# One power for four tiles in the band's query and key norm, and two gate products issued beside the last heads

## The chip, the cores and the metric

The kernel runs on one core of a Trainium2 chip. The metric is the device time of one execution in microseconds (us), the median of three runs. The engines are named as in the profile: PE is TensorE (its matmuls; PEld its weight loads), DVE is VectorE, ACT is ScalarE, POOL is GpSimd, SP is SyncE, which issues most DMAs.

## What is computed

Two transformer layers act on one sequence of 512 tokens with width 1024. The change lies in the second layer, whose mixer has two halves of width 512:

```python
qa, ka, va, qkv_b, z_b, b_raw, a_raw = jnp.split(proj, cuts, axis=-1)
o_a = chunked_band_attention(qa, ka, va, q_gain, k_gain, rel_bias)   # 8 heads of 64, rms norm of q and k per head
o_a = rms_norm_2(o_a, attn_out_gain)
o_b = gated_delta_rule(q_b, k_b, v_b, g, beta)                       # 4 heads of 128
o_b = rms_norm_2(o_b, dn_out_gain) * jax.nn.silu(z_b)                # z_b: the gate
mix = jnp.concatenate([o_a, o_b], axis=-1) @ w_out
x = x + gate1 * mix
```

The norm of q and k is x times (mean(x*x) + eps) to the power -0.5, for each token and head. After this a mixture of 16384 single-neuron experts follows, which takes the second half of the kernel's time.

## The kernel before

Activations lie as 512 tokens in four tiles of 128 (`NT = 4`). Large products run in three passes of a rounded format: each weight block of 128x1024 numbers is loaded (SP queue, four buffers `wr`), rounded to a high part `wh` on ACT (L51) and its remainder `wl` computed on DVE, or on POOL where the caller passes `eng` (L52; three buffers each). `gemm_t` (L76) then issues 24 matmuls of 512 columns (L72 to L74) into one of four PSUM buffers named `g`. `gemm_n` (L87) gives the four tiles side by side, with a callback `mid` every second tile (L98 to L100).

Every engine executes its instructions in a fixed order. That order isn't the order of the text: a planner reorders at build time. It takes, on each engine, the instruction that stands earliest in the text among those that its own estimate of times shows ready and for which a buffer is free. On the chip the engine then waits wherever an instruction isn't ready, with all that is queued behind it.

The stages around the change, in the order of the text:

- `band_pre` (L1176) makes the band's q (j=0) and k (j=1). For each, a `gemm_n` of 512 columns, then per tile: copy to SBUF on ACT (L1201), square (L1203) and sum (L1205) on DVE, scale and eps (L147, in `rstd_small`), power on POOL (L151; tiles `bn_v`, `bn_r`, one buffer each), and the product on DVE (L1207). After j=1 a `gemm_n` of 256 columns for the values (`w_va1`). The transposes of the normed tiles are L1188.
- `dn_tile` (L997), two of them at once (tiles 2 and 3), are steps that `mid` releases between the products of `band_pre`: each call of `mid(n)` adds n to a debt and issues one step for each whole unit of it. There are 19 steps; twelve of them alternate L1064 (a product with `Ub`, which POOL makes, L1060), copies and transposes (L1066, L1053, L1054), and L1073 with a subtraction on DVE into `X` (L1074), on which the next L1064 waits. The last one is L1078 to L1086. The debts sum to 18 by the end of `band_pre`; what is left follows in a loop (L916).
- `dn_scan` (L1100), twelve steps, and `band` (L1215), 32 steps, are issued in turn, two of the band for one of the scan. A step of the band is one tile of one head: scores into a buffer `g` (L1230), `soft` (L543): maximum on DVE (L548), exponential on ACT (L552), reciprocal and product on DVE (L554, L555), transposes on PE (L559), copy on ACT (L561), product with the values on PE (L563). Every second head ends with a copy (L1235), a square on ACT (L204) and a sum on POOL (L206). After the scan eight steps are left, the last two heads. The band's end is a sum over channels (L114), a power (L151), a broadcast (L136, L138) and four products (L1241).
- `zb` (L1088) makes the four gate products, `gemm_t` of `w_zb`, with a tanh on ACT (L1094) and a product on DVE (L1096) each. The text issues the first after the band's end; `pair` (L243) then splits the band's four results, `dn_out` (L1162) transposes and gates the scan's (L1170, L1172), between the other three; then `out2` (L1249) multiplies with `w_o2`.

Of the kernel before, what the change touches and what calls it, by code (L numbers as in the profile page):

```python
# [8 lines left out]
F32 = mybir.dt.float32  # L9
# [6 lines left out]
OP = mybir.AluOpType  # L16
AX = mybir.AxisListType
# [3 lines left out]
P = 128  # L21
T = 512
NT = 4
# [3 lines left out]
class Kernel:  # L27
# [860 lines left out]
    def layer2(self, st0):  # L888
        tc, nc, I = self.tc, self.nc, self.i
        cp, mod2 = self.cp, self.mod2  # L890
        with ExitStack() as st:
            lp = self.lp = st.enter_context(tc.tile_pool(name="lp", bufs=1, reuse_waits="tile"))
            G = self.gains[0]
            nc.vector.scalar_tensor_tensor(G, mod2[:, 8:16], 1.0, G, op0=OP.add, op1=OP.mult)
            with tc.tile_pool(name="hp2", bufs=1, side="right", reuse_waits="tile") as hp:
                hs = [(self.t(hp, [P, T], F32R, f"hh{k}"), self.t(hp, [P, T], F32R, f"hl{k}")) for k in range(8)]
                with tc.tile_pool(name="np2", bufs=1, reuse_waits="tile") as np2:
                    self.norm_mod(np2, self.x1, hs, G, mod2[:, 0:8], self.ss)
                sd = ExitStack()
                self.dk = sd.enter_context(tc.tile_pool(name="dk", bufs=1, reuse_waits="tile"))  # L900
                with tc.tile_pool(name="dp", bufs=1, reuse_waits="tile") as self.dp:
                    self.dn_pre(hs)
                    for _ in self.dn_tiles([0, 1]):
                        pass
                    tiles = self.dn_tiles([2, 3])
                    self.owed = 0.0

                    def mid(n):

                        self.owed += n  # L910
                        while self.owed >= 1.0:
                            self.owed -= 1.0
                            next(tiles, None)

                    self.band_pre(hs, mid)
                    for _ in tiles:  # L916
                        pass
                with tc.tile_pool(name="bp", bufs=1, side="right", reuse_waits="tile") as bp:
                    self.bp = self.ap = bp
                    scan, band = self.dn_scan(), self.band()  # L920
                    zb = self.zb(hs)
                    for _ in scan:
                        next(band)
                        next(band)
                    for _ in band:
                        pass
                    next(zb)
                    parts = [self.pair(bp, x, "pr", "pts", 4) for x in self.oa]
                    out = self.dn_out()
                    for _ in zb:  # L930
                        next(out)
                    for _ in out:
                        pass
                    sd.close()
                    self.out2(parts)
# [152 lines left out]
    def zb(self, hs):  # L1088
        nc = self.nc
        self.zzb = []  # L1090
        for h in range(4):
            z = self.gemm_t(self.i["w_zb"][h], 8, hs)
            tz = self.t(self.bp, [P, T], F32, "tz", 2)
            nc.scalar.activation(tz, z, AF.Tanh, scale=0.5)  # L1094
            zz = self.t(self.lp, [P, T], F32, f"zzb{h}")
            nc.vector.scalar_tensor_tensor(zz, tz, 1.0, z, op0=OP.add, op1=OP.mult)  # L1096
            self.zzb.append(zz)
            yield
# [77 lines left out]
    def band_pre(self, hs, mid):  # L1176
        nc, I, lp, dp = self.nc, self.i, self.lp, self.dp
        G = nc.gpsimd
        gq = self.load(dp, "attn_qk_g", [P, 2])
        nc.vector.tensor_scalar(gq[:, 0:1], gq[:, 0:1], 0.125, None, op0=OP.mult)  # L1180
        sh = [P, 8, 64]
        self.aT = [self.t(self.ep, [P, 4, T], F32, f"e{j}") for j in range(2)]

        def trans(j, xs):
            for t in range(NT):
                p = self.t(self.pa, [P, T], F32, "a")
                for b in range(4):
                    nc.tensor.transpose(p[:, b * P:b * P + P],  # L1188
                                        xs[t][:, 2 * b:2 * b + 2].rearrange("p h d -> p (h d)"), self.ident)
                nc.scalar.activation(self.aT[j][:, :, t * P:t * P + P], p.rearrange("p (b x) -> p b x", b=4), AF.Copy,  # L1190
                                     scale=gq[:, j:j + 1])

        xs = None
        for j, w in enumerate(("w_qa", "w_ka")):
            ps = self.gemm_n(I[w], 512, hs, mid=lambda: mid(0.8))
            if j:
                trans(0, xs)
            xs = []
            for t in range(NT):
                x = self.t(dp, sh, F32, "cv_u" if t % 2 else "cv_t", 2)  # L1200
                nc.scalar.activation(x, ps[t].rearrange("p (h d) -> p h d", h=8), AF.Copy)  # L1201
                sq = self.t(dp, sh, F32, "qn_d", 1)
                nc.vector.tensor_mul(sq, x, x)  # L1203
                s = self.t(dp, [P, 8], F32, "bn_s", 2)
                nc.vector.tensor_reduce(s, sq, axis=AX.X, op=OP.add)  # L1205
                r = self.rstd_small(dp, s, 1.0 / 64, "bn")
                nc.vector.tensor_mul(x, x, r.unsqueeze(2).to_broadcast(sh))  # L1207
                xs.append(x)
        ps = self.gemm_n(I["w_va1"], 256, hs, mid=lambda: mid(0.65))
        for t in range(NT):  # L1210
            nc.scalar.activation(self.va[:, t, 256:], ps[t], AF.Copy)
        with self.tc.issue_after(self.mm.ins):
            trans(1, xs)
# [514 lines left out]
def host_layout(inp):  # L1728
# [47 lines left out]
    w2 = a["w_in_2"][0]  # L1776
    o = np.cumsum([0, 512, 512, 512, 1536, 512, 4, 4])
    qa, ka, va, qkv, zb, b_, a_ = [w2[:, o[j]:o[j + 1]] for j in range(7)]
    r["w_va0"] = wn(np.concatenate([va[:, :256], b_, a_], 1))
    r["w_va1"] = wn(va[:, 256:])  # L1780
    r["w_qa"], r["w_ka"] = wn(qa), wn(ka)
    r["w_qkv"], r["w_zb"] = wt(qkv), wt(zb)
    r["dn_conv"] = np.ascontiguousarray(a["dn_conv_w_2"][0].reshape(4, 12, P).transpose(2, 1, 0))
    r["dn_dt_bias"], r["dn_a_log"] = row(a["dn_dt_bias_2"][0]), row(a["dn_a_log_2"][0])
# [34 lines left out]
```

## Time and profile before

| | before |
|---|---|
| median of three runs | 2485.56 us (2482.98 to 2485.98) |
| profiled execution, its time | 2485.87 us |
| profiled execution, its span | 2483.2 us |
| PE busy | 2391.6 us, 96% of the span |
| DVE, ACT, POOL busy | 75%, 42%, 28% |
| granted TensorE clock, mean | 0.989 |
| `band_pre` | about 960 to 1076 us |
| scan and band | about 1076 to 1159 us |
| gate products and `out2` begin | 1140 us and 1177 us |

The span is what lies between the first and the last instruction; 2.7 us of the execution lie around it. A busy PE isn't a PE at its peak: a matmul counts as busy for as long as it lasts, also at half clock. The granted clock of a stretch is the mean of its two levels, 1.0 for 2.4 GHz and 0.5 for 1.2 GHz.

### The profile page before, as it was taken

The page shows a single profiled execution, that of the slowest core. Times are in us where ns is not written, and L with a number is a line of the kernel's source. Part 1 is how long each engine was busy: PE and PEld are TensorE (multiplying, and loading weights), DVE is VectorE, ACT ScalarE, POOL GpSimd, SP SyncE. Part 2 cuts the span into 40 slices and gives each one's busy share as a digit, 9 for nine tenths or more (in the row PEclk, how much of TensorE's full clock was granted, in tenths as well). Part 3 has the DMA queues.
Part 4 walks back from the last instruction along what each step waited for, and adds up shares of the span by engine and source line. Part 5 has one row for each costly group of instructions (what it writes and reads, how often), then busy time and mean ns, then how long its engine had stood idle before and what let it go on. Part 6 is the DMA issues. An engine that isn't in the chain of part 4 may idle for free.

```text
span 2483.2 us, 34683 instructions
## 1 busy us (share of the span) xinstructions
PE 2391.6 (96%) x12573; PEld 2021.0 (81%) x12573; DVE 1867.6 (75%) x3610; ACT 1046.0 (42%) x1871; POOL 704.4 (28%) x526
## 2 busy tenths in 40 slices
PE   5998999999999999999999999999999999999999
PEld 4786777778788778876788999999978888888887
DVE  7895677777765575565458889989668888888887
ACT  3444466653322434354444344454433333333332
POOL 0250111120000112421344665211224344444431
PEclk9999999999999999999999999999999999999999
DMA  7222212228865310111422565889989999999996
GB/s 258 77 85 77 77 55 82 81 73 292 291 224 192 122 68 31 39 60 47 134 77 85 191 198 184 299 310 340 324 278 345 342 348 347 350 348 335 354 353 245
DMA packets 197579, 497.66 MB, mean 200 GB/s; under 512 B 19872, under 2 KB 83872, under 8 KB 194336
## 3 DMA queue, kind: packets, MB, share of 16 engines
q1 hardware_dynamic: 157088, 336.06, 39.9%
q0 software_dynamic: 36864, 134.23, 14.9%
q10 hardware_dynamic: 3456, 25.17, 2.6%
q8 instruction: 98, 1.61, 0.3%
q14 instruction: 73, 0.60, 0.1%
HBM read 446.63 MB, written 48.76 MB: 200 GB/s over the span
## 4 chain that ended last, share of the span: by engine, by line
PE 71%; DVE 13%; DMA 6%; issue 4%; POOL 3%; ACT 2%; SPq 0%; DVEq 0%; POOLq 0%; ACTq 0%
PE g L72 14%; PE g L74 13%; PE g L73 13%; PE acc L72 5%; PE acc L73 5%; PE acc L74 5%; DVE wl L52 2%; PE a L563 2%; DMA wr<-in_w_up 1%; DMA row<-in_rows_up,idx 1%; DVE cv_u L576 1%; PE a L1616 1%; PE a L1617 1%; PE a L559 1%; PE g L98 1%
## 5 line engine op out<-in xcount | busy, mean ns | idle before, releaser
L51 ACT ACTIVATE wh<-wr 128x1024 fp32r<-128x1024 f32 (+2 forms) x424 | 442.9, 1046 | 588.0 <-PE g L73 289.6
L72 PE MATMUL g<-hh,wh 128*128 128x384 f32 (+1 forms) x1792 | 657.0, 367 | 7.3 <-ACT act L1653 5.7
L74 PE MATMUL g<-hh,wl 128*128 128x384 f32 (+1 forms) x1792 | 651.5, 364 | 3.3 <-POOL wl L52 3.2
L73 PE MATMUL g<-hl,wh 128*128 128x384 f32 (+1 forms) x1792 | 651.5, 364 | 0.0
L52 DVE TENSOR_TENSOR wl<-wr,wh 128x1024 fp32r<-128x1024 f32 (+3 forms) x351 | 428.5, 1223 | 119.7 <-ACT wh L51 115.9
L72 PEld LDWEIGHTS g<-hh,wh 128*128 128x128 f32 x1792 | 337.5, 188 | 41.8 <-ACT act L1653 7.8
L74 PEld LDWEIGHTS g<-hh,wl 128*128 128x128 f32 x1792 | 337.6, 188 | 39.3 <-POOL wl L52 4.7
L73 PEld LDWEIGHTS g<-hl,wh 128*128 128x128 f32 x1792 | 337.7, 188 | 33.9 <-issue 4.7
L73 PE MATMUL acc<-wl,gh 128*128 128x512 f32 x768 | 299.7, 390 | 4.3 <-DVE wl L52 4.3
L74 PE MATMUL acc<-wh,gl 128*128 128x512 f32 x768 | 299.2, 390 | 0.0
L72 PE MATMUL acc<-wh,gh 128*128 128x512 f32 x768 | 297.4, 392 | 1.4 <-ACT wh L51 1.4
L1690 POOL DMA_INDIRECT row<-in_rows_dn,idx x128 | 167.9, 1312 | 374.6 <-DVE row L1696 348.9
L1690 POOL DMA_INDIRECT row<-in_rows_up,idx x128 | 177.5, 1386 | 222.1 <-DVE h2n L1715 189.9
L52 POOL TENSOR_TENSOR wl<-wr,wh 128x1024 fp32r<-128x1024 f32 x73 | 181.3, 2490 | 193.2 <-ACT wh L51 184.8
L51 ACT ACTIVATE gh<-ga 128x384 fp32r<-128x384 f32 x128 | 67.2, 525 | 314.4 <-issue 135.4
L1715 DVE SCALAR_TENSOR_TENSOR h2n<-row,gw,h2n 128x1024 f32<-128x1024 f32 x127 | 162.8, 1282 | 16.5 <-DMA row<-in_rows_up,idx 15.4
L73 PEld LDWEIGHTS acc<-wl,gh 128*128 128x128 f32 x768 | 144.4, 188 | 36.1 <-DVE wl L52 6.0
L72 PEld LDWEIGHTS acc<-wh,gh 128*128 128x128 f32 x768 | 144.6, 189 | 32.3 <-ACT wh L51 2.5
L1696 DVE SCALAR_TENSOR_TENSOR row<-row,h2n 128x1024 f32<-128x1024 f32 x128 | 159.2, 1256 | 13.1 <-DMA row<-in_rows_dn,idx 13.1
L74 PEld LDWEIGHTS acc<-wh,gl 128*128 128x128 f32 x768 | 144.3, 188 | 29.9
L98 PE MATMUL g<-wh,hh 128*128 128x512 f32 (+3 forms) x256 | 96.9, 381 | 12.4 <-ACT hh L227 12.0
L880 DVE SCALAR_TENSOR_TENSOR wr<-wr,sc 128x1024 f32<-128x1024 f32 x56 | 68.0, 1223 | 42.3 <-DMA wr<-in_ada_w 42.0
(547 smaller groups left out, 3809.3 us busy)
## 6 DMA issues: line engine op xcount, KB each, us to landing
wr<-in_w_dn SPq DMA_DIRECT2D x128, 512.0 KB, 5.1
wr<-in_w_up SPq DMA_DIRECT2D x128, 512.0 KB, 8.1
wr<-in_ada_w SPq DMA_DIRECT2D x56, 512.0 KB, 4.6
g_d<-stage ACTq DMA_DIRECT2D x24, 1024.0 KB, 8.5
gr<-g_d SPq DMA_DIRECT2D x32, 768.0 KB, 11.7
wr<-in_w_x SPq DMA_DIRECT2D x24, 512.0 KB, 3.5
act_d<-act SPq DMA_DIRECT2D x56, 192.0 KB, 4.1
ar<-act_d SPq DMA_DIRECT2D x56, 192.0 KB, 7.4
```

What stands on the lines that cost most here:

```text
L51: nc.scalar.activation(hi, src, AF.Copy)
L52: eng.tensor_sub(lo, src, hi.bitcast(F32))
L72: mm(ps, ah, bh, start=first, stop=False)
L73: mm(ps, ah, bl, start=False, stop=False)
L74: self.mm = mm(ps, al, bh, start=False, stop=last)
L98: mm(pss[t], hh[:, tt], wh[:, k], start=f, stop=False)
L559: nc.tensor.transpose(pt[:, sb * P:sb * P + P], pr[:, sb * P:sb * P + P], self.ident)
L563: nc.tensor.matmul(o, vsb(sb), pts[:, sb * P:sb * P + P], start=sb == 0, stop=sb == n - 1)
L880: nc.vector.scalar_tensor_tensor(w, w, 1.0, cur[cname], op0=OP.mult, op1=OP.mult, accum_out=acc[:, b:b + 1])
L1690: nc.gpsimd.indirect_dma_start(r, None, src, bass.IndirectOffsetOnAxis(ap=self.idx[:, s:s + 1], axis=0))
L1696: nc.vector.scalar_tensor_tensor(r, r, 1.0, self.h2n, op0=OP.mult, op1=OP.mult, accum_out=act[:, s:s + 1])
L1715: nc.vector.scalar_tensor_tensor(acc, r, w[:, s:s + 1], acc, op0=OP.mult, op1=OP.add)
```

## The change

In `band_pre` the sums of squares of the four tiles go into one tile `bn_s` of 32 columns, one `rstd_small` takes one power for all of them, one more unit of debt is added behind it (`mid(1.0)`, twice in all), and the four products follow. In the run over the last two heads of the band, the first gate product is issued after the first step (head 6, tile 0), the second after the fifth (head 7, tile 0), instead of behind the band's end. The weight remainders of these two go to POOL instead of DVE. The loop that issues a step of `dn_out` behind every further gate product now does so two times instead of three.

```diff
@@ layer2
                     for _ in scan:
                         next(band)
                         next(band)
-                    for _ in band:
-                        pass
-                    next(zb)
+
+                    for n, _ in enumerate(band):
+                        if n in (0, 4):
+                            next(zb)
                     parts = [self.pair(bp, x, "pr", "pts", 4) for x in self.oa]
@@ zb
-            z = self.gemm_t(self.i["w_zb"][h], 8, hs)
+            z = self.gemm_t(self.i["w_zb"][h], 8, hs, eng=nc.gpsimd if h < 2 else None)
@@ band_pre
             xs = []
+
+            s = self.t(dp, [P, NT * 8], F32, "bn_s", 1)
             for t in range(NT):
                 x = self.t(dp, sh, F32, "cv_u" if t % 2 else "cv_t", 2)
                 nc.scalar.activation(x, ps[t].rearrange("p (h d) -> p h d", h=8), AF.Copy)
                 sq = self.t(dp, sh, F32, "qn_d", 1)
                 nc.vector.tensor_mul(sq, x, x)
-                s = self.t(dp, [P, 8], F32, "bn_s", 2)
-                nc.vector.tensor_reduce(s, sq, axis=AX.X, op=OP.add)
-                r = self.rstd_small(dp, s, 1.0 / 64, "bn")
-                nc.vector.tensor_mul(x, x, r.unsqueeze(2).to_broadcast(sh))
+                nc.vector.tensor_reduce(s[:, t * 8:t * 8 + 8], sq, axis=AX.X, op=OP.add)
                 xs.append(x)
+            r = self.rstd_small(dp, s, 1.0 / 64, "bn")
+
+            mid(1.0)
+            for t, x in enumerate(xs):
+                nc.vector.tensor_mul(x, x, r[:, t * 8:t * 8 + 8].unsqueeze(2).to_broadcast(sh))
```

## Rows read from the trace of the kernel before

**Rows 1.** The page, part 1: busy time, share, instructions.

```profile
PE 2391.6 (96%) x12573; PEld 2021.0 (81%) x12573; DVE 1867.6 (75%) x3610; ACT 1046.0 (42%) x1871; POOL 704.4 (28%) x526
```

**Rows 2.** Busy by stretch: length, PE, PEld, DVE, ACT, POOL, clock, DMA share, GB/s.

```profile
2000.00:2300.00 300.00, 297.65 (x1419) 259.12 (x1418) 255.14 (x297) 108.80 (x149) 134.24 (x96) 1.00 0.98 346
```

**Rows 3.** PE's waits at 995:1020 and 1040:1078: total us, times, longest.

```profile
PE a L1064 <- DVE X L1074: 0.7, 2, 0.5
...
PE a L1064 <- DVE bn_v L147: 4.2, 2, 2.5
```

**Rows 4.** Timeline, 1040:1056: start, us, engine, line, operation [idle before it].

```profile
1040.68 1.00 DVE L1203 TENSOR_TENSOR qn_d<-cv_t 128x512 f32<-128x512 f32 x1 [2.11 <-ACT cv_t L1201]
...
1044.77 1.95 PE L1073 MATMUL a<-Z,Y 128*128 128x128 f32 x16
...
1049.28 0.69 DVE L1207 TENSOR_TENSOR cv_u<-cv_u,bn_r 128x512 f32<-128x512 f32 x1 [1.53 <-POOL bn_r L151]
...
1050.48 0.68 DVE L1074 TENSOR_TENSOR X<-X,a 128x512 f32<-128x512 f32 x1
...
1051.31 1.13 PE L1064 MATMUL a<-X,Ub 128*128 128x128 f32 x8 [1.72 <-DVE bn_v L147]
...
1054.57 0.68 DVE L1074 TENSOR_TENSOR X<-X,a 128x512 f32<-128x512 f32 x1
```

**Rows 5.** Busy by stretch, the 5 us around that wait's end.

```profile
1055.00:1060.00 5.00, 4.61 (x26) 4.64 (x27) 3.47 (x5) 1.20 (x2) 4.53 (x3) 0.66 0.34 108
```

**Rows 6.** Busy by stretch over the last two heads and the band's end.

```profile
1130.00:1140.00 10.00, 7.51 (x29) 3.45 (x27) 5.59 (x24) 4.70 (x13) 3.32 (x3) 0.87 0.00 0
1140.00:1152.00 12.00, 11.71 (x69) 8.33 (x69) 4.76 (x22) 5.49 (x16) 0.00 (x0) 0.83 0.01 1
1152.00:1159.00 7.00, 5.84 (x27) 4.05 (x27) 1.59 (x3) 2.77 (x4) 2.29 (x2) 1.00 0.00 0
```

**Rows 7.** Timeline, 1130:1141: the scan's end on DVE, scores, first gate matmul.

```profile
1134.14 0.69 DVE L1157 TENSOR_TENSOR qkv<-qkv,sc_r 128x512 f32<-128x512 f32 x1 [1.19 <-POOL sc_r L151]
...
1135.10 1.79 PE L1230 MATMUL g<-e,e 64*128 64x128 f32 x6 [1.10 <-DVE mx L548]
...
1140.29 0.80 PE L72 MATMUL g<-hh,wh 128*128 128x512 f32 x1 [0.39 <-DVE mx L548]
```

**Rows 8.** POOL's powers by shape: count, busy us, mean ns, idle before.

```profile
L151 POOL TENSOR_TENSOR bn_r<-bn_v,mhalf 128x8 f32<-128x8 f32 x8 | 15.4, 1920 | 13.5 <-DVE bn_v L147 13.4
...
L151 POOL TENSOR_TENSOR hr_r<-hr_v,mhalf 128x16 f32<-128x16 f32 x2 | 5.8, 2906 | 32.0 <-DVE hr_v L147 32.0
...
L151 POOL TENSOR_TENSOR sc_r<-sc_v,mhalf 128x4 f32<-128x4 f32 x4 | 4.0, 1011 | 4.7 <-DVE sc_v L147 3.5 <-DVE nm L550 1.2
```

**Rows 9.** Timeline, 1057:1060: a product on DVE beside two on POOL.

```profile
1057.38 2.73 POOL L1060 TENSOR_TENSOR Ub<-U,lm 128x512 f32<-128x512 f32 x2
1057.45 1.63 DVE L1207 TENSOR_TENSOR cv_u<-cv_u,bn_r 128x512 f32<-128x512 f32 x1 [1.53 <-POOL bn_r L151]
```

**Rows 10.** PE's groups by shape, 1046.4:1070: the value product (one of three lines).

```profile
L98 PE MATMUL g<-wh,hh 128*128 128x256 f32 x24 | 7.4, 307 | 0.0
```

**Rows 11.** Timeline, 1150:1178: last values product to the first of `out2`.

```profile
1150.96 1.09 PE L563 MATMUL a<-pts,va 128*64 128x128 f32 x8
...
1156.76 0.39 PE L73 MATMUL g<-hl,wh 128*128 128x512 f32 x1
1156.98 0.40 PE L74 MATMUL g<-hh,wl 128*128 128x512 f32 x1
...
1162.64 0.69 DVE L52 TENSOR_TENSOR pts<-qkv,pr 128x512 fp32r<-128x512 f32 x1
...
1177.10 0.48 PE L72 MATMUL g<-pr,wh 128*128 128x512 f32 x1
```

**Rows 12.** The page, part 5: weight remainders on DVE and on POOL.

```profile
L52 DVE TENSOR_TENSOR wl<-wr,wh 128x1024 fp32r<-128x1024 f32 (+3 forms) x351 | 428.5, 1223 | 119.7 <-ACT wh L51 115.9
L52 POOL TENSOR_TENSOR wl<-wr,wh 128x1024 fp32r<-128x1024 f32 x73 | 181.3, 2490 | 193.2 <-ACT wh L51 184.8
```

## The prediction

> **What bounds the kernel now.** First the page's busy shares: PE is busy 96% of the span [rows 1], so the time is PE's work plus the few places where PE waits or runs slowly. Then the busy times by stretch, to see whether a gain in the middle reaches the end: from 2000 to 2300 us PE is busy 297.65 of 300 us [rows 2], and nothing there is tied to a clock time, so an earlier start should come through whole. Then PE's waits in the two places that the diff touches. In `band_pre` PE loses 0.7 us (j=0) and 4.2 us (j=1) before L1064 [rows 3]. The timeline tells why. The wait is booked on `bn_v`, but L1064 reads `X`, and the subtraction L1074 that makes `X` stands on DVE behind a norm product L1207, which stands still for 1.53 us until POOL's power is there: L1207 at 1049.28, L1074 at 1050.48, L1064 at 1051.31; the other tile's L1074 follows only at 1054.57, behind the next product [rows 4]. After this idle stretch PE's mean clock is 0.66 over 5 us [rows 5]: 0.34 / 0.5 x 5 = 3.4 us at 1.2 GHz, in which half, 1.7 us, is lost.
>
> At the band's end PE is idle 2.5, 0.3 and 1.2 us in the stretches 1130:1140, 1140:1152 and 1152:1159, and the clocks 0.87 and 0.83 [rows 6] mean 2.6 + 4.1 = 6.7 us at 1.2 GHz; about 6 of these are busy, and half of that, 3.0 us, is lost. Together 4.0 + 3.0 = 7.0 us. The cause: the scan's last product on DVE, held by POOL's power, ends at 1134.8; only then do the maxima of head 6 free score buffers, and the scores of head 7 start at 1135.10. The first gate matmul comes at 1140.29, when another score buffer falls free [rows 7]: the planner already pulls it ahead of the band's end, but the text's order gives the buffers `g` to the scores first.
>
> All that is to be had is 0.7 + 4.2 + 1.7 + 7.0 = 13.6 us, 0.55% of the time.
>
> **Part A, one power for four tiles.** Removed for each j: three L147 and three L151. A power takes 1.01 us for 4 columns and 2.91 for 16 [rows 8]: 0.158 us a column over 0.38. For 32 columns that is an estimate of 5.4 us. The eight powers of 8 columns took 1.92 us each instead of the 1.64 of this line [rows 8]; scaled alike, 6.4 us. Four of them cost 7.7 us today, so POOL gains 1.3 to 2.3 us for each j. But DVE, which today waits 1.53 us four times, waits once for 5.4 to 6.4 us, less what the planner puts in between: above all the `X` subtractions, which `mid(1.0)` issues ahead of the products at j=1.
>
> I follow j=1. Squares and sums, eight instructions of 512 columns at 0.69 us, run from 1040.7 to 1046.2, the power from some 1046.5 to 1052. L1073 of this level ends at about 1046.6 [rows 4], so both L1074, ahead of the products, are done by 1048 instead of 1051.2 and 1055.2. L1064 then follows without a wait: the 4.2 us and the 1.7 us of clock go. What is late next is the level after: its `Ub` on POOL stands behind the power, its L1074 behind the four products (1052 to some 1056.5, since a product that ran beside `Ub` took 1.63 us and not 0.69 [rows 9, 4]). To lie over the 10 us from 1046.5 PE has the rest of the value product, 3 x 24 matmuls [rows 10] of half the 0.22 us that 512 columns take [rows 11], 8 us, and some 5 us of L1064, L1053 and L1073. How the planner deals them out is open, and PE then waits 0 to 3 us, with the clock's half on top. I take half of 5.9 us as kept: 2.9, between 0 and 5.5. At j=0 the wait of 0.7 us has the same cause, and the product of 512 columns lies over the power: 0.7 us go, between -1 and +0.7. The two added units of debt bring `dn_tile`'s steps forward and add no instruction. **A gives 3.5 us**, -1 to 6.
>
> **Part B, two gate products beside heads 6 and 7.** Nothing is added or removed: 48 matmuls move up, with two tanh on ACT and two products on DVE, and two remainders go from DVE (1.22 us) to POOL (2.49 us) [rows 12]. The two weight loads on SP's queue pass the bias loads of the last two heads in the text; the planner puts them ahead of the band already today, where the four buffers `wr` allow it, so I cost them at nothing; if a bias came late for it, one wait of a few us at head 6 would follow. POOL's 5.0 us fall between the power and the first scores. A matmul follows the last after 0.22 us [rows 11], so a product is 5.4 us. Of the first one's 24, 15 come behind the last product with the values (1150.96), the last at 1156.98 [rows 11]; all of the second come behind it. In the new text the first stands ahead of the scores of tiles 1 to 3 of head 6. PE then has work while DVE waits for the scan's power, and the clock has no reason to fall.
>
> How far does it come through? The last product with the values ends at 1152.05; the first split result of the band is there at 1163.3, so the chain behind it takes 11.3 us; but `out2` starts at 1177.10 [rows 11], 13.8 us later than this chain asks. So `out2` waits for PE's work, not for the band, and idle time removed ahead counts whole. Left behind the band are two gate products, 11 us, and some 3.5 us of sums, broadcast and transposes: 14.5 us over a chain of 11.3, enough. The 1.2 us idle in 1152:1159 stay, since PE waits there for the band's sum and broadcast in the order of its queue. Of 7.0 us I take 5.5, between 0 (the hole stays) and 7. DVE loses 2.4 us of splits; nothing waits for that. `dn_out`'s last two steps now both follow the fourth gate product; their inputs are ready since 1134.8. **B gives 5.5 us.**
>
> **The sum**: 3.5 + 5.5 = 9.0 us off the profiled execution's 2485.87, whose span is 2483.2; it stands 0.3 us over the median of 2485.56. From the median: 2476.5 us.
>
> **POOL's longer instructions, weighed.** A norm product that started on DVE 0.07 us after a POOL product of 512 columns took 1.63 us instead of 0.69 [rows 9, 4]. The Trainium skill, page "SBUF — State Buffer", section "SBUF: two separate sides", says that DVE and GpSimd share a port pair, which the first comer holds for its whole instruction against a DVE instruction with two SBUF inputs. By that rule, with which this row agrees, a split of 2.49 us can hold DVE as long. What that would cost here is in rival 2.
>
> **The rivals.** (1) *Only B works.* The planner thinks the power short and puts the products ahead of `X` on DVE, or one `X` ahead and one behind. Then L1064 waits until 1052 + 4 x 0.69 = 1054.8 instead of 1051.3 and 1055.2: A gives -1 to +1, the time is 2480. For it: L1074 stands behind L1207 today by the same estimates [rows 4]. Against it: today each `X` slipped in where DVE had a gap, and a longer power makes a longer gap. (2) *Only A works.* The gate matmuls take the place of scores that PE runs ahead of the hole today, and the hole stays, because the scores of head 7 still wait for maxima behind the scan's power. B gives 0 to 2: 2481.5. The same time comes if POOL's two splits each hold DVE for 2.49 us on the chain, 5.0 of the 9 us. (3) *It does nothing*: the planner's order hardly changes, since it already takes the gate product forward, to 1140.29; 2485. (4) *Slower.* The gate product holds one of four score buffers from its first matmul until DVE has read it, and its 24 matmuls stand ahead of three scores. If DVE and ACT run dry meanwhile, each of the two heads ends up to 5.4 us later and the holes stay behind. 13.8 us of slack less the 9 us (39 matmuls) that no longer lie behind the band: it decides from 5 us of delay of the band's end. With 2 x 5.4 = 11 us `out2` starts 6 us later, and with A at 0 the time is 2491.5. For it: three buffers feed a pipeline that had four. Against it: DVE is busy only 5.59 of 10 and 4.76 of 12 us there [rows 6], and while it waits for the scan it could not use the scores.
>
> **How the numbers follow.** Both parts work: 0.50, 2471 to 2480, likeliest 2476.5. Only B: 0.15, 2478 to 2482. Only A: 0.13, 2480 to 2484. Nothing: 0.10, 2483 to 2488. Slower: 0.12, 2488 to 2493. A measurement of this kernel can tell 0.2%, 5 us, from no change: below 2480.6, above 2490.5. Faster by more: 0.50 and half of "only B", 0.58. Slower by more: most of the last case, 0.10. Same: 0.32. The range 2470 to 2487 leaves out "slower", the top of "nothing" and what lies beyond the best case, under 0.2.
>
> **What would show it.** A is right if the timeline has one L151 of 128x32 for each j of 5.4 to 6.4 us with L1074 ahead of it or within it, and the waits of L1064 behind it sum to under 3 us. B is right if the first two gate products end before the last L563, if the clock stays at 1.0 over the last two heads, and if `out2` starts some 9 us earlier. It would be wrong if DVE's next `X` stood behind the four products with PE idle for over 4 us, or if the scores of heads 6 and 7 waited for a free `g`.

## The result: slower by 0.68%

| | before | after |
|---|---|---|
| median of six runs | 2483.28 us (2480.87 to 2485.98) | 2501.18 us (2497.16 to 2504.27) |
| ratio, 95% interval | | 1.0068 (1.0056 to 1.0079) |
| profiled execution, its span | 2483.2 us | 2499.2 us |
| granted TensorE clock, mean | 0.989 | 0.980 |
| first matmul of `w_qa` | 934.04 us | 933.93 us |
| first scores of the band | 1076.02 us | 1086.56 us |
| first matmul of `out2` | 1177.10 us | 1192.17 us |

The change was forecast to gain 9 us and lost 17. The last three rows, each the start of one line in the timeline, say where: from `w_qa` to the first scores (`band_pre`) it takes 152.63 us instead of 141.98, 10.6 more; from there to `out2` (the band) 105.61 instead of 101.08, 4.5 more; behind `out2` nothing changes that can be told (1307.0 and 1306.1 us). In what follows, lines of the changed file count one higher than before in `dn_tile` (L1064 is L1065, L1073 is L1074, L1074 is L1075, L1084 is L1085); the four products are L1213, the bias loads L1230 and the scores L1235.

PE's work is the same. Part 1 of the page of after, to be held against [rows 1]: PE's busy time is 11.7 us higher with the same 12573 matmuls, so they were slower, at a lower clock; the other 4.3 us by which the span grew are idle time.

```profile
PE 2403.3 (96%) x12573; PEld 2031.9 (81%) x12573; DVE 1866.0 (75%) x3602; ACT 1045.5 (42%) x1871; POOL 706.5 (28%) x522
```

PE's waits of after at 995:1078, against the 0.7 and 4.2 us of [rows 3] (total, times, longest):

```profile
PE a L1065 <- DVE X L1075: 12.8, 2, 7.4
```

Timeline of after around the first of these waits, at j=0 (start, us, engine, line, operation, idle before it):

```profile
1005.55 1.23 DVE L52 TENSOR_TENSOR wl<-wr,wh 128x1024 fp32r<-128x1024 f32 x1
1005.70 6.34 POOL L151 TENSOR_TENSOR bn_r<-bn_v,mhalf 128x32 f32<-128x32 f32 x1 [1.56 <-DVE bn_v L147]
1006.16 1.95 PE L1074 MATMUL a<-Z,Y 128*128 128x128 f32 x16
...
1010.45 0.39 PE L100 MATMUL g<-wh,hl 128*128 128x512 f32 x1
...
1012.08 1.63 DVE L1213 TENSOR_TENSOR cv_t<-cv_t,bn_r 128x512 f32<-128x512 f32 x1 [5.31 <-POOL bn_r L151]
...
1015.44 1.27 DVE L1075 TENSOR_TENSOR X<-X,a 128x512 f32<-128x512 f32 x2
1016.26 0.98 PE L1065 MATMUL a<-X,Ub 128*128 128x128 f32 x3 [5.42 <-DVE X L1075]
```

The second matmul of the level, L1074, ends at 1008.1, so `X` could be subtracted then. But on DVE the four products stand ahead of it, and the first of them stands still for 5.31 us until the power is there. PE has one block of twelve matmuls to lay over this (to 1010.8), then it waits 5.42 us. The same at j=1, with more on top:

```profile
1057.61 5.42 POOL L151 TENSOR_TENSOR bn_r<-bn_v,mhalf 128x32 f32<-128x32 f32 x1 [1.56 <-DVE bn_v L147]
1062.99 2.34 POOL L52 TENSOR_TENSOR wl<-wr,wh 128x1024 fp32r<-128x1024 f32 x1
1063.06 2.82 DVE L1213 TENSOR_TENSOR cv_t<-cv_t,bn_r 128x512 f32<-128x512 f32 x1 [5.53 <-POOL bn_r L151]
1065.80 0.68 DVE L1213 TENSOR_TENSOR cv_u<-cv_u,bn_r 128x512 f32<-128x512 f32 x1
...
1067.61 1.27 DVE L1075 TENSOR_TENSOR X<-X,a 128x512 f32<-128x512 f32 x2
1068.42 0.98 PE L1065 MATMUL a<-X,Ub 128*128 128x128 f32 x3 [7.40 <-DVE X L1075]
```

The first product takes 2.82 us instead of 0.68, beside a remainder of a gate weight on POOL. At the start of the band there is a third stall, which before doesn't have. Timeline of before, then of after:

```profile
1072.01 0.90 SPq L1225 DMA_DIRECT2D bias<-in_rel_bias  x2
1072.27 1.14 PE L1078 MATMUL a<-vn,Y 128*128 128x128 f32 x8
...
1076.64 0.29 DVE L548 CUSTOM_DVE_ANT_0 pr<-g,bias 128x128 f32<-128x128 f32 x1 [0.71 <-PE g L1230]
```

```profile
1069.93 17.61 SPq L65 DMA_DIRECT2D wr<-in_w_o  x3
...
1079.39 1.06 PE L1079 MATMUL a<-vn,Y 128*128 128x128 f32 x8
...
1085.96 1.23 DVE L52 TENSOR_TENSOR wl<-wr,wh 128x1024 fp32r<-128x1024 f32 x1 [3.00 <-ACT wh L51]
1086.56 2.92 PE L1235 MATMUL g<-e,e 64*128 64x128 f32 x8 [0.25 <-ACT e L1191]
1087.59 0.90 SPq L1230 DMA_DIRECT2D bias<-in_rel_bias  x2
...
1092.26 0.29 DVE L548 CUSTOM_DVE_ANT_0 pr<-g,bias 128x128 f32<-128x128 f32 x1 [5.08 <-POOL bias L1231]
```

(A row with x3 is three issues merged; the third load of `w_o2` goes out at 1087.21.) In both kernels the bias loads stand on SP's queue behind the third load of `w_o2`, which waits for a `wr` buffer, and this comes free with a weight remainder on DVE at the end of the value product: the rounding that the remainder needs stands on ACT behind the last copy of the values. Before, the last step of `dn_tile` (L1078, L1084, from 1072.27 to 1076.02) lies between that moment and the first scores, and covers the load of some 4 us. After, it stands at 1079.39, ahead of the value product's end, the scores follow at once, and the first maximum waits 5.08 us for the bias.

Busy by stretch of after (length, PE, PEld, DVE, ACT, POOL, clock, DMA share, GB/s): each stall is followed by a stretch at 0.50 to 0.83, in which a busy PE does between half and five sixths of its work.

```profile
1015.00:1020.00 5.00, 3.74 (x17) 3.77 (x18) 2.85 (x4) 1.19 (x2) 1.15 (x1) 0.50 0.13 39
1020.00:1025.00 5.00, 5.00 (x24) 4.41 (x23) 0.00 (x0) 1.20 (x2) 1.16 (x1) 0.83 0.05 17
...
1090.00:1095.00 5.00, 2.38 (x6) 1.89 (x7) 2.71 (x17) 1.59 (x5) 0.29 (x2) 0.50 0.31 104
1095.00:1100.00 5.00, 4.51 (x11) 1.85 (x11) 1.64 (x8) 1.67 (x7) 0.14 (x1) 0.50 0.18 52
...
1145.00:1180.00 35.00, 34.80 (x188) 24.58 (x187) 17.00 (x57) 15.77 (x39) 3.49 (x4) 1.00 0.19 60
```

The last row is the gates' part at work: the hole of [rows 6] is gone, PE is busy 34.80 of 35 us at full clock over the last heads.

### The profile page after: what moved, and what is told of

Same layout as the page of the kernel before. It is cut to its first block, busy times and chain, and to the rows that moved or that the text cites. A ratio compares the mean times of both kernels' runs of the same rounds, so it can differ in the third digit from the quotient of the medians.

```text
span 2499.2 us, 34668 instructions
## 1 busy us (share of the span) xinstructions
PE 2403.3 (96%) x12573; PEld 2031.9 (81%) x12573; DVE 1866.0 (75%) x3602; ACT 1045.5 (42%) x1871; POOL 706.5 (28%) x522
## 4 chain that ended last, share of the span: by engine, by line
PE 73%; DVE 12%; DMA 6%; issue 4%; POOL 3%; ACT 2%; SPq 0%; DVEq 0%; POOLq 0%; ACTq 0%
PE g L72 13%; PE g L74 13%; PE g L73 13%; PE acc L72 5%; PE acc L73 5%; PE acc L74 5%; DVE wl L52 2%; PE a L563 2%; DMA wr<-in_w_up 1%; PE g L98 1%; PE g L99 1%; PE g L100 1%; POOL row L1695 1%; DMA row<-in_rows_dn,idx 1%; PE a L1065 1%
## 5 line engine op out<-in xcount | busy, mean ns | idle before, releaser
L52 POOL TENSOR_TENSOR wl<-wr,wh 128x1024 fp32r<-128x1024 f32 x75 | 187.3, 2503 | 210.1 <-ACT wh L51 201.7
L52 DVE TENSOR_TENSOR gl<-ga,gh 128x384 fp32r<-128x384 f32 x128 | 70.9, 554 | 43.3 <-ACT gh L51 40.1
```

The costliest lines, as they stand in the source:

```text
L52: eng.tensor_sub(lo, src, hi.bitcast(F32))
```

## The experiments

My first theory was that the norm's part loses all of it, by the order on DVE (about 10 us) and by the late bias (about 7), and that the gates' part gains some 4. Its rivals: the bias is late because of the gates' weights; the gates' part loses too. All runs are compared with runs of before on the same chip. The lengths are read in each run's profile as in the table above.

| run | median, us | ratio to before (95%) | `band_pre`, us | band, us |
|---|---|---|---|---|
| before | | 1 | 141.98 | 101.08 |
| after | 2501.18 | 1.0068 (1.0056 to 1.0079) | 152.63 | 105.61 |
| e1_only_norm | 2500.94 | 1.0062 (1.0046 to 1.0078) | 149.07 | 111.39 |
| e2_only_gates | 2481.41 | 0.9982 (0.9974 to 0.9991) | 141.96 | 95.39 |
| e3_no_debt | 2483.21 | 0.9994 (0.9986 to 1.0003) | 143.60 | 100.87 |
| e4_x_first | 2487.40 | 1.0005 (0.9994 to 1.0016) | 140.40 | 104.02 |
| e5_last_step | 2491.30 | 1.0033 (1.0021 to 1.0044) | 152.46 | 95.40 |
| e6_bias_pool | 2492.45 | 1.0032 (1.0019 to 1.0044) | 149.93 | 98.52 |
| e7_debt_j1 | 2482.42 | 0.9995 (0.9984 to 1.0005) | 142.47 | 95.40 |
| e8_gates_bias | 2479.56 | 0.9980 (0.9971 to 0.9989) | 141.91 | 96.49 |
| e9_x_first_j1 | 2478.31 | 0.9971 (0.9961 to 0.9982) | 136.65 | 97.99 |
| e10_four_powers | 2476.43 | 0.9966 (0.9954 to 0.9979) | 136.49 | 98.23 |
| e11_gates_dve | 2481.45 | 0.9990 (0.9981 to 0.9999) | 140.38 | 96.48 |
| e12_norm_no_debt | 2481.45 | 0.9986 (0.9975 to 0.9997) | 137.53 | 102.32 |
| f1_no_debt_dve | 2477.54 | 0.9965 (0.9954 to 0.9976) | 137.58 | 97.74 |
| f2_after_dve | 2500.70 | 1.0053 (1.0040 to 1.0067) | 150.52 | 106.82 |
| f3_x_first_dve | 2478.19 | 0.9964 (0.9950 to 0.9977) | 136.36 | 96.66 |

The medians of before on these chips lie between 2483.28 and 2486.56 us, so the runs are set against each other by their ratios. A length is read in one execution, and the clock isn't the same in each. In e3_no_debt PE is busy 9.48 us from 1080 to 1090 at a clock of 0.66, in e7_debt_j1 9.43 us at 1.00, both at the start of the band. So the band of 100.87 us in e3's row is not a price of that kernel; its profiled execution took 3.3 us more than its median.

### The two parts alone, and the debt

**e1_only_norm** is the change without its two edits for the gates, **e2_only_gates** these two alone:

```diff
-                    for _ in band:
-                        pass
-                    next(zb)
+                    for n, _ in enumerate(band):
+                        if n in (0, 4):
+                            next(zb)
-            z = self.gemm_t(self.i["w_zb"][h], 8, hs)
+            z = self.gemm_t(self.i["w_zb"][h], 8, hs, eng=nc.gpsimd if h < 2 else None)
```

> The norm's part alone (one power for four tiles, with its two units of debt); the gate products stand as before. Theory: the loss is all here. X stands behind the four products and these behind one power of 5.4 to 6.3 us (first scores 10.5 us later in the changed kernel than before), and the two units of debt take the last step of dn_tile away from behind the value product, so that the bias comes late (a wait of 5 us on DVE, with the clock some 7.5 us). 2483.3 + 10.5 + 7.5 = 2501, between 2498 and 2504. Rival: the bias is late because of the gates' part (two remainders on POOL, on which SP's queue waited 11.3 us): then only the 10.5 us are left, 2493 to 2495.

> The gates' part alone: two gate products beside the last heads, with two remainders on POOL; the norm as before. Theory: it gains what the last heads show in the changed kernel (PE without a hole from 1105 to 1180), 3 to 5 us: 2478 to 2481. Rival: the gate products hold score buffers and the POOL remainders delay SP's queue, so that this part loses too: 2488 or more.

Both as the theory has it: 1.0062 and 0.9982. The norm's part alone has the same three stalls; the first maximum waits 4.88 us for the bias, though its gate remainders are on DVE. The gates' part alone brings `out2` 5.7 us nearer to the first scores; its median lies 0.4 us over my range.

**e3_no_debt** is the changed kernel without one line:

```diff
-            mid(1.0)
```

> The changed kernel without the two added units of debt. Theory: the products still stand ahead of X behind the long power, so band_pre loses about 10 us as in the changed kernel; but the last step of dn_tile stands behind the value product again and covers the load of the bias, so that the 7.5 us go and the gates' gain of 4 us shows: 2483.3 + 10.5 - 4 = 2490, between 2487 and 2493. Rival: the debt doesn't matter, the bias is late because the value product ends late: 2499 to 2502.

Here my theory fell. I had expected the products' place ahead of `X` to keep 10 us of loss; the time is 2483.2, and `band_pre` is only 1.6 us longer than before. So the two units of debt cost all of the loss, the late bias and most of the price that I had put on the order. At j=0 0.6 us of waiting are left, as in before (0.7); at j=1 there is one wait of 5.00 us.

**e4_x_first** orders the products behind `X` at both j, with more debt:

```diff
-            V.tensor_sub(D, D, p)
+            self.xs = V.tensor_sub(D, D, p)
-            mid(1.0)
-            for t, x in enumerate(xs):
+            mid(2.0)
+            with self.tc.issue_after(self.xs.ins):
+                for t, x in enumerate(xs):
-        ... mid=lambda: mid(0.65))
+        ... mid=lambda: mid(0.25))
```

> The changed kernel with two units of debt more behind each power's scale and the four products ordered behind the X subtraction of that level; the value product's debts are cut from 0.65 to 0.25, so that the last step of dn_tile stays behind it. Theory (what costs is the order on DVE, not the power): no wait of L1064's successor behind the products at j=1, the bias in time, the gates' gain of 4 us: 2475 to 2481. Rival (the long power costs wherever X stands, since Ub waits behind it on POOL): 2488 or more.

2487.4, between the two, and its runs lie far apart (2478.9 to 2493.9). The waits for `X` are down to 0.4 us, but the rival's mechanism is there at j=0, where `Ub` waits behind the power (PE's waits at 995:1082):

```profile
PE a L1065 <- POOL Ub L1061: 2.9, 1, 2.9
```

and in its profiled execution the bias still came 3.25 us late. Too many things moved at once for this run to settle more.

### What the debt does: the last step and the first unit

**e5_last_step** keeps both units of debt and takes as much away from the value product, so that the debts sum to 18 as before:

```diff
-        ... mid=lambda: mid(0.65))
+        ... mid=lambda: mid(0.4))
```

**e6_bias_pool** leaves the debts and takes the bias loads out of SP's queue:

```diff
-                nc.sync.dma_start(bias, I["rel_bias"][h])
+                (nc.gpsimd if h < 2 else nc.sync).dma_start(bias, I["rel_bias"][h])
```

> The changed kernel with its two units of debt, but the value product's debts cut from 0.65 to 0.4, so that the debts sum to 18 again and the last step of dn_tile stands behind the value product as before. Theory: the bias is late in the changed kernel because that step no longer lies over its load; with it back, DVE's wait of 5.08 us at the first maximum and the half clock behind it go, the stalls of X at j=0 and j=1 stay: 2501.2 - 7.5 = 2493.5, between 2491 and 2496. Rival: the bias is late because the third load of w_o2 stands ahead of it in SP's queue, wherever the step stands: 2499 to 2503.

> The changed kernel with the bias loads of heads 0 and 1 issued from POOL's queue instead of SP's, where they stood behind the third load of w_o2. Theory: they are issued as soon as dn_tile's memory is free, at some 1083 instead of 1087.6, DVE's wait falls from 5.08 us to about 1 and the half clock behind it shrinks: 4 to 7 us less, 2494 to 2497. Rival: the memory or POOL's own queue holds them as long: 2499 to 2503.

Both theories hold, and they agree with each other: 2491.3 and 2492.5, some 9 us less than after, by two quite different edits that have only the bias in common (for the second I had expected 4 to 7; it lies 1.5 us below my range). The bias load and the first maximum, first of e5_last_step, then of e6_bias_pool:

```profile
1081.42 0.90 SPq L1230 DMA_DIRECT2D bias<-in_rel_bias  x2
...
1086.05 0.29 DVE L548 CUSTOM_DVE_ANT_0 pr<-g,bias 128x128 f32<-128x128 f32 x1 [0.71 <-PE g L1235]
```

```profile
1080.65 1.39 POOL L1230 DMA_DIRECT2D bias<-in_rel_bias  x2
...
1086.54 0.29 DVE L548 CUSTOM_DVE_ANT_0 pr<-g,bias 128x128 f32<-128x128 f32 x1 [0.29 <-POOL bias L1231]
```

The wait of 5.08 us is 0.71 and 0.29. So the bias came late because the debts had pulled the last step of `dn_tile` ahead of the value product's end. That is shown.

**e7_debt_j1** then drops the unit at j=0 alone:

```diff
-            mid(1.0)
+            if j:
+                mid(1.0)
-        ... mid=lambda: mid(0.65))
+        ... mid=lambda: mid(0.525))
```

> As the kernel with 0.4, but the unit of debt stands at j=1 alone, and the value product's debts are 0.525 (sum 18 again). Theory: the unit at j=0 is what puts the next step of dn_tile on PE ahead of the product that lay over the power; without it j=0 has no wait (the kernel without both units shows 5.00 of 5 us busy from 990 to 1015), and j=1 waits about 5 us as that kernel does: 2483 to 2487, and 8 us under the kernel with 0.4 and both units. Rival: each unit costs alike: 2488 to 2491.

2482.4 (0.6 us below my range), 9 us less than e5_last_step, as the theory says. PE's waits at 995:1110, first of e5_last_step, then of e7_debt_j1:

```profile
PE a L1065 <- DVE X L1075: 12.1, 2, 6.7
```

```profile
PE a L1065 <- DVE X L1075: 6.0, 3, 5.3
```

The wait of 5.4 us at j=0 is down to 0.7 in two pieces, and the one at j=1 is 1.4 us shorter. The timeline of e7_debt_j1 at j=0 shows why, against the one of after:

```profile
1011.59 1.95 PE L1074 MATMUL a<-Z,Y 128*128 128x128 f32 x16
1013.29 0.48 PE L98 MATMUL g<-wh,hh 128*128 128x512 f32 x1
...
1018.60 0.39 PE L100 MATMUL g<-wh,hl 128*128 128x512 f32 x1
1019.53 0.68 PE L1065 MATMUL a<-X,Ub 128*128 128x128 f32 x4 [0.55 <-DVE X L1075]
```

The order on DVE is the same, `X` behind the four products. But between L1074 and the next L1065 PE now has 24 matmuls of the product (1013.29 to 1019.0, 5.7 us) instead of twelve (1007.86 to 1010.8, 3.0 us), since the step comes later in the text. The unit of debt took away the cover and left the wait.

**e8_gates_bias** is e2_only_gates with e6_bias_pool's edit.

> The gates' part alone, with the bias loads of heads 0 and 1 on POOL's queue. Theory: there the first maximum waits only 0.71 us for the bias, so that an earlier load brings at most 1 us: 2480 to 2482. Rival: the start of the band hangs on the bias by more than this wait shows (the second head's bias comes 1.8 us after the first): 2478 or less. Third case: two more transfers issued by POOL hold its memory work: 2484 or more.

0.9980 against 0.9982: where the bias is in time, an earlier load brings nothing that can be told (the median is 0.4 us under my range).

### The order at j=1, and the number of powers

**e9_x_first_j1** is e4_x_first with the debt at j=1 alone (the order stays at both j):

```diff
-            mid(2.0)
+            if j:
+                mid(3.3)
-        ... mid=lambda: mid(0.25))
+        ... mid=lambda: mid(0.24))
```

**e10_four_powers** is e2_only_gates with the four powers of before; only at j=1 the products leave the loop and stand behind `X` (with 0.24 in the value product):

```diff
-                r = self.rstd_small(dp, s, 1.0 / 64, "bn")
-                nc.vector.tensor_mul(x, x, r.unsqueeze(2).to_broadcast(sh))
+                r = self.rstd_small(dp, s, 1.0 / 64, f"bn{t}" if j else "bn")
+                rs.append(r)
+                if not j:
+                    nc.vector.tensor_mul(x, x, r.unsqueeze(2).to_broadcast(sh))
                 xs.append(x)
+            if j:
+                mid(3.3)
+                with self.tc.issue_after(self.xs.ins):
+                    for x, r in zip(xs, rs):
+                        nc.vector.tensor_mul(x, x, r.unsqueeze(2).to_broadcast(sh))
```

> The changed kernel with no debt behind the power at j=0 and 3.3 units at j=1, the four products ordered behind the X subtraction of that level, and the value product's debts 0.24 (sum 18, last step where it was). Theory: what is left of the norm's loss is the order on DVE at j=1; without it the wait of 5.3 us and the half clock behind it (0.66 over 5 us, 1.7 us) of the kernel with 0.525 go: 2482.4 - 6 = 2476.5, between 2474 and 2479. Rival: Ub, which waits behind the long power on POOL (2.9 us in the kernel that orders X first in both), takes the place of the wait: 2480 to 2483.

> The gates' part, with four powers as before, but at j=1 the four products are taken out of the loop and ordered behind the X subtraction, with 3.3 units of debt ahead and 0.24 in the value product. Theory: the wait of L1064 (4.2 us) and its half clock (1.7 us) come from the order on DVE and not from the number of powers, so they go here too: 2481.4 - 6 = 2475.5, between 2473 and 2478, the same as with one power. Rival: one power is what matters: 2480 to 2483 here.

Both theories hold: 0.9971 and 0.9966, and `band_pre` is 5.3 and 5.5 us shorter than before, with one power or with four. PE's waits of e9_x_first_j1 at 995:1072 begin with

```profile
PE a L1065 <- DVE X L1075: 1.1, 3, 0.5
```

and this row is the same in e10_four_powers. What costs at j=1 is `X` behind a product that waits for a power, not how many powers there are. By the ratios alone the step from e2_only_gates to e10_four_powers, 4 us, is at the edge of the noise; it is the lengths and the waits that show it. The order and the debt at j=1 were changed together in both runs, so what the order brings without more debt isn't shown. Both kernels are faster than before and after.

### POOL's remainders beside the norm's products

**e11_gates_dve** is e2_only_gates with the remainders on DVE, **e12_norm_no_debt** is e1_only_norm without the debt:

```diff
-            z = self.gemm_t(self.i["w_zb"][h], 8, hs, eng=nc.gpsimd if h < 2 else None)
+            z = self.gemm_t(self.i["w_zb"][h], 8, hs)
```

```diff
-            mid(1.0)
```

> The gates' part with the two weight remainders on DVE as before instead of POOL. Theory: they lie off the path on either engine (DVE is busy 5.6 of 10 us in the band): no difference from the gates' part, 2480 to 2483. Rival (POOL's two remainders each hold DVE on the path): 2476 to 2478. Third case (DVE's remainders of 1.22 us stand ahead of maxima): 2484 or more.

> The norm's part alone and without the two units of debt: one power for four tiles and nothing else. Theory: at j=1 X still stands behind the products, these behind the power, and PE waits 5.0 us instead of 4.2, with more of the half clock behind it; the kernel without debt and the kernel with the gates alone stand 1.8 us apart (2483.2 and 2481.4), so this is 1 to 4 us slower than before: 2486 to 2489. Rival: the power itself gains (POOL does 5.4 us instead of 7.7 for each j) and the 1.8 us are scatter: 2481 to 2485.

e11_gates_dve shows no difference that can be told from e2_only_gates, as expected. e12_norm_no_debt doesn't do what I had expected: one power alone, without the debt, is a little faster than before (0.9986, the interval ends at 0.9997), within the rival's range. Then the norm (0.9986) and the gates (0.9982) each gain alone, yet together, in e3_no_debt, they gain nearly nothing (0.9994). The timelines at j=1 tell what they do to each other, first e3_no_debt, then e12_norm_no_debt:

```profile
1047.50 5.42 POOL L151 TENSOR_TENSOR bn_r<-bn_v,mhalf 128x32 f32<-128x32 f32 x1 [4.03 <-DVE bn_v L147]
...
1052.89 1.16 POOL L1061 TENSOR_TENSOR Ub<-U,lm 128x512 f32<-128x512 f32 x1
1052.96 1.64 DVE L1212 TENSOR_TENSOR cv_t<-cv_t,bn_r 128x512 f32<-128x512 f32 x1 [4.94 <-POOL bn_r L151]
1054.00 2.85 POOL L52 TENSOR_TENSOR wl<-wr,wh 128x1024 fp32r<-128x1024 f32 x1
1054.51 2.88 DVE L1212 TENSOR_TENSOR cv_u<-cv_u,bn_r 128x512 f32<-128x512 f32 x1
...
1058.88 2.82 DVE L1212 TENSOR_TENSOR cv_u<-cv_u,bn_r 128x512 f32<-128x512 f32 x1
1061.63 1.27 DVE L1075 TENSOR_TENSOR X<-X,a 128x512 f32<-128x512 f32 x2
1062.45 1.83 PE L1065 MATMUL a<-X,Ub 128*128 128x128 f32 x7 [5.00 <-DVE X L1075]
```

```profile
1057.57 1.63 DVE L1211 TENSOR_TENSOR cv_t<-cv_t,bn_r 128x512 f32<-128x512 f32 x1 [4.94 <-POOL bn_r L151]
1059.13 1.65 DVE L1211 TENSOR_TENSOR cv_u<-cv_u,bn_r 128x512 f32<-128x512 f32 x1
1060.70 0.68 DVE L1211 TENSOR_TENSOR cv_t<-cv_t,bn_r 128x512 f32<-128x512 f32 x1
1061.31 0.68 DVE L1211 TENSOR_TENSOR cv_u<-cv_u,bn_r 128x512 f32<-128x512 f32 x1
...
1063.87 1.13 PE L1064 MATMUL a<-X,Ub 128*128 128x128 f32 x8 [1.80 <-DVE X L1074]
```

With the gates' remainders on POOL the four products take some 9 us (1052.96 to 1061.7), without them 4.4 (1057.57 to 1062.0), and PE's wait is 5.00 us instead of 1.80. Each held product ends some 0.5 us after the POOL instruction beside it (1054.60 after 1054.05, 1057.39 after 1056.85). The Trainium skill, page "SBUF — State Buffer", section "SBUF: two separate sides", has the rule that the prediction weighed: DVE and GpSimd share a port pair, and the one that starts first holds it for its whole instruction, against a DVE instruction with two SBUF inputs, where GpSimd's reads SBUF. These rows agree with it.

Three more runs were made for this. **f1_no_debt_dve** is the changed kernel less the debt and less POOL's remainders:

```diff
-            mid(1.0)
-            z = self.gemm_t(self.i["w_zb"][h], 8, hs, eng=nc.gpsimd if h < 2 else None)
+            z = self.gemm_t(self.i["w_zb"][h], 8, hs)
```

**f2_after_dve** has the second of these edits alone, **f3_x_first_dve** is e9_x_first_j1 with it.

> The changed kernel without the two units of debt and with the gates' two remainders on DVE. Theory (the two parts disturb each other: a remainder on POOL holds the norm's product on DVE): at j=1 the four products took 1.64, 2.88, 1.64 and 2.82 us beside POOL's Ub and remainders, and 1.63, 1.65, 0.68 and 0.68 without remainders; PE's wait falls from 5.0 to about 2 us and its half clock goes: 2483.2 - 5 = 2478, between 2476 and 2480.5. Rival (the remainders are covered; the gap between the kernel without debt and the norm alone without debt is scatter): 2482 to 2485.

> The changed kernel with the gates' two remainders on DVE, nothing else. Theory: at j=1 the first product no longer takes 2.82 us beside POOL's remainder but about 0.7, so that PE's wait of 7.4 us falls by 2; the stall at j=0 (5.4 us) and the late bias stay: 2501.2 - 2.5 = 2498.7, between 2497 and 2500. Rival: the remainder on DVE stands ahead of the last subtractions and the maxima: 2500 to 2504.

> The kernel with X ordered first at j=1 and no debt at j=0, with the gates' remainders on DVE. Theory: with X ahead of the products nothing on the path waits for them, so that a product of 2.87 us beside a remainder costs nothing and its removal brings nothing: 2477 to 2480 as with the remainders on POOL. Rival: it gains as the other kernel does: 2474 to 2476.

f1_no_debt_dve: 0.9965, 2477.5 us. The two parts together gain as much as their sum alone, when the debt and POOL's remainders are gone; PE's waits at 995:1072 are

```profile
PE a L1065 <- DVE X L1075: 2.5, 3, 1.8
```

f2_after_dve: the product and the wait at j=1 shrink as expected, to 0.69 and 5.28 us, and the stall at j=0 and the late bias (4.64 us) stay. Its median, 2500.7, lies in the rival's range and 0.7 us above mine; its ratio, 1.0053, is a little under that of after with intervals that overlap. So the time neither shows nor excludes the 2.5 us.

```profile
1064.58 0.69 DVE L1213 TENSOR_TENSOR cv_t<-cv_t,bn_r 128x512 f32<-128x512 f32 x1 [5.53 <-POOL bn_r L151]
...
1067.83 2.05 PE L1065 MATMUL a<-X,Ub 128*128 128x128 f32 x8 [5.28 <-DVE X L1075]
```

f3_x_first_dve: 0.9964, no difference from e9_x_first_j1 (0.9971): with `X` ahead of the products their length doesn't matter.

**The loss put together**, by the ratios, each times 2485 us, with some 4 us of uncertainty on a difference: both parts without the debt and with the remainders on DVE -8.7 (f1_no_debt_dve); with POOL's remainders -1.5 (e3_no_debt), which costs 7; with the unit of debt at j=1 -1.2 (e7_debt_j1), nothing; with the unit at j=0 as well +8.2 (e5_last_step), 9 more; with the last step pulled ahead of the value product's end +16.9 (after), 9 more. The parts don't simply add. The debt's line costs 18 us beside POOL's remainders (e3_no_debt to after), 22 without them (f1_no_debt_dve to f2_after_dve) and 19 in the norm alone (e12_norm_no_debt to e1_only_norm). The remainders cost 7 us without the debt, but 4 with it (f2_after_dve to after), which can't be told from nothing. No run has the debt with the four powers of before, so how much of its price needs the long power isn't shown.

## Why the prediction was wrong

**The debt, costed at nothing, is the step that failed.** "The two added units of debt bring `dn_tile`'s steps forward and add no instruction" is true, and I took it for a price of zero without naming the work that each step had covered. It was 18 of the 26 us between forecast and result (18 to 22, by the run that is compared). The first unit moved L1065 one block of twelve matmuls nearer to the power. My sentence on j=0, that the product of 512 columns lies over the power, holds in e7_debt_j1 and not in after; the lower end that I gave it, -1 us, was taken from the wait of 0.7 us of [rows 3], though it should have come from the power and four products, 5.4 + 4 x 0.7 us, less the one block that stays. Together the units ended `dn_tile` a step earlier, and that last step was the cover of the bias load. I did write that a late bias would cost a wait of a few us, but I looked for it at head 6, from the gates' weights; it came at head 0, from the debt. A row would have shown it: in before the bias is issued at 1072.01, takes some 4 us, and is used at 1076.64.

**POOL's remainders.** I wrote that their 5.0 us "fall between the power and the first scores". They do, and just there the norm's products stand. It cost 7 us in the step from f1_no_debt_dve to e3_no_debt; in their traces 6.0 us of this lie in `band_pre`, 3.2 of it in PE's wait at j=1. The second half of rival 2 had this mechanism, with 5.0 us; what was wrong is that I gave it no place in the sum, though the rows for it were before me [rows 9].

**Part A.** The power took 5.42 us and 6.34 us, near the two bounds that I had worked out from [rows 8]; the upper one by luck, since the 0.9 us more stand beside a DVE remainder (1005.55) and not in a scaled price. That `X` of the level goes ahead of the products at j=1 was right, but not for the reason that I gave, the debt: it does so in e12_norm_no_debt and e3_no_debt, which have none. That the next level's would be late, by 0 to 3 us, was right too for the norm alone: 1.80 us. `band_pre` was then 4.5 us shorter (137.53 against 141.98), where I had 3.5. In after, with remainder and debt on top, PE's wait was 7.40 us. What I hadn't seen is that the number of powers isn't what matters: e10_four_powers gains as much with four.

**Part B** was right in mechanism and nearly in size: 5.5 us forecast, and the band is 5.7 us shorter in e2_only_gates and 4.6 in e11_gates_dve, with ratios that give 4.5 and 2.5 us of the whole. The gate products fill the hole, `out2` starts 12.3 us after the last product with the values ends in e11_gates_dve (1158.7 and 1171.0; from [rows 11] I had read that this chain needs 11.3), and the 1.2 us at the band's sum that I let stand are there in after as well: "PE a L114 <- POOL bsq L206: 1.2".

**The rivals.** The slower one, a gate product that holds a score buffer, did not happen (in e2_only_gates PE waits 0.3 us for one from 1085 to 1185); the slower result came by another road, which I hadn't written down as a rival, only as a sign of being wrong: DVE's next `X` behind the four products and PE idle for over 4 us. That sign showed twice. "Only B works" had the products ahead of `X` too, but priced it at -1 to +1 us, without POOL's remainder and without the clock behind the wait.

**The sum.** 9.0 us was forecast for the two parts; without the debt and POOL's remainders they gave 8.7 (6.0 to 11.4 by the interval of f1_no_debt_dve). The idea's price held, and that of what stood beside it did not. That the two are so near is in part luck: the 2.9 us in part A were half of a range, taken for want of a better number, and alone the two parts came out at 3.5 us and at 2.5 to 4.5.

## What to carry to other kernels

A moved step that adds no instruction still takes its cover away with it: for every step that comes earlier, name what it lay over before (a load, a power, a wait), and price that as if it were bare. When a short wait on an in-order engine is traded for one long wait, look at what stands behind it in the queue and put the urgent work first; the order mattered here, the number of instructions did not. Work sent to POOL "beside" something should be checked against the two-input DVE instructions of the same microseconds.

## What the runs showed of the hardware

- The hold between DVE and POOL goes both ways. A product of 0.68 us on DVE took 1.64 beside a POOL product of 1.16 and 2.82 to 2.88 beside a remainder of 2.34 to 2.85; and the power of 5.42 us took 6.34 where a DVE remainder of 1.23 us had started 0.15 us before it. The subtraction `X`, one of whose inputs lies in PSUM, isn't held: it took 0.69 us in the middle of the power (timeline of e9_x_first_j1).

```profile
1049.48 5.42 POOL L151 TENSOR_TENSOR bn_r<-bn_v,mhalf 128x32 f32<-128x32 f32 x1
1050.76 0.69 DVE L1075 TENSOR_TENSOR X<-X,a 128x512 f32<-128x512 f32 x1 [1.35 <-PE a L1074]
```

- A wait of 5 us on PE cost some 8 us in after: behind the one of 5.42 us the clock was 0.50 for 5 us and 0.83 for 5 more, so that 3.74 us and 0.34 x 5 = 1.7 us of busy time did half the work, 2.7 us on top. What comes on top differs between executions: worked out in the same way it is 2.9 us behind the 5.00 us in e3_no_debt and 1.5 behind the 5.25 us in e7_debt_j1. In e3_no_debt the clock also stood at 0.50 from 1082 to 1088 where PE had been idle for 0.5 us; in e7_debt_j1 it stayed at 1.00 behind as short an idle time at the same place.
- The first bias load issued by POOL was there 5.7 us after its issue (1080.65 to 1086.36, e6_bias_pool). Those issued by SP took from 3.9 us (e5_last_step, 1081.42 to 1085.37) to 5.7 (e4_x_first, 1077.82 to 1083.53), so these runs show no difference between the queues.
